# Interleaved hi and lo blocks, backward weight columns and a 64-byte shift in a PE-filled four-layer trunk

## The chip, the cores and the metric

The kernel runs on one core of a Trainium2 chip. The metric is the device time of one launch, in microseconds; less is better. Two timed runs of the kernel before took 2014.99 and 2016.04 us, a median of 2015.51 us.

## The reference

The input is one sequence of 256 frames with 2048 features. Two layers follow each other: a token mixer and an MLP in each, every one of the four behind an RMSNorm and with a residual add.

```python
for i in range(DEPTH):                         # DEPTH = 2
    h = rms_norm(x, norm_mix[i])
    x = x + (stick_breaking_mixer if i == 0 else dsa_mixer)(h, ...)   # 16 heads of 128
    h = rms_norm(x, norm_mlp[i])
    x = x + jnp.square(jax.nn.relu(h @ w_up[i])) @ w_down[i]          # 2048 -> 8192 -> 2048
```

The first mixer projects to q, k, v (2048 to 6144), weighs keys by stick breaking and projects back (2048 to 2048). The second projects to 16 query heads, 4 key and 4 value heads and an indexer (16 heads of 64), keeps the 64 best keys of each query, and projects back. Nearly all the arithmetic lies in the products of 256 frames with weight matrices; the inputs and the result are float32.

## The kernel before, in words

**Products.** Every float32 operand is split in two float32r parts, hi and lo, and a product is the sum of three: hi with hi, lo with hi, hi with lo. The frames are the stationary operand of TensorE (128 features by 128 frames, loaded by a LDWEIGHTS ahead of each MATMUL), the weight matrix is the moving one (128 features by 512 columns). One *item* is a block of 256 rows (KB = 2 k tiles of 128) by 512 columns of a weight matrix, 512 KB. An item in the plain form has 12 matmuls: 2 halves of the frames, 2 k tiles, 3 part products. A list of 882 items is worked off in order; each is loaded by SyncE into `wraw` (five buffers), split by ScalarE into `wh` (line 1327) and by VectorE into `wl` (line 1328), two items ahead of its matmuls.

**Where products stand.** `tokens_out` (matmuls in line 342, and in line 333 for the first two items) makes a group of 512 output columns from eight items, q = 0 to 7, of which q reads k tiles 2q and 2q + 1. There are 16 such groups over the normed features `xT` (four in the first mixer, two in each MLP, eight in the second mixer) and 8 in the two output projections, over `oT`. `seven_products` makes two columns of items at once: for some q a scheme of seven products in place of eight is used (line 465), and the others are plain products (line 446). With one set of the scheme these are q = 1, 3, 4, 5, 6, 7, with two sets q = 4 to 7; the k tiles from 8 on are never in the scheme, and `sums` adds up k tiles 0 to 7 alone. `xT` is the left operand of 18 such calls, four in the first mixer and seven in each MLP; 8 of them use one set and 10 two. The second product of an MLP reads the squared features from `half` (three buffers of 8 k tiles) and the sums of these from `S` and `S2`.

**Features.** `xT` has 16 k tiles; in each lie 256 hi values and then 256 lo values, so that a stationary block is 128 consecutive float32 values (512 bytes in a partition). They are written by ScalarE (hi) and VectorE (lo) with 256 values an instruction: `prep_first` (lines 188 and 189) for the first layer, `turn_steps` (lines 255 and 260) for the three later ones, at the seams between the four sections. The indexer's key product (`ki_part`, lines 1047 and 1048) is the one place where `xT` is the moving operand, with 80 weight columns as the stationary one.

**Addresses.** Some tiles named `pad` fill up space. With them the build puts `xT`, `wh`, `wl`, `wraw`, `half`, `S`, `S2`, `X`, `Y` and `Z` at multiples of 512 bytes in a partition. In the second mixer, `vh` and `vl` lie 128 bytes past such a multiple, and `ph` and `pl` 224 bytes past; `o_step` (lines 1244 to 1246) multiplies these.

Of the kernel before, what the change touches and what calls it, by code (L numbers as in the profile page):

```python
# [9 lines left out]
F32 = mybir.dt.float32  # L10
F32R = mybir.dt.float32r
BF16 = mybir.dt.bfloat16
AF = mybir.ActivationFunctionType
OP = mybir.AluOpType
# [3 lines left out]
P = 128  # L18
D = 2048
S = 256  # L20
KT = D // P
# [18 lines left out]
KB = WT // 512  # L40
# [15 lines left out]
BIAS = 60  # L56
ROLES = {
    "mixer": ("G0 H0 s1 G1 s3 H1 G2 s6 H2 s5 G3 s7 H3 s2 G4 H4 s4 G5 H5", dict(
        T1a=1, T2a=3, T3a=5, T4a=11, P1=5, P6=7, P5=10, P7=11)),
# [38 lines left out]
class Item:  # L98
# [3 lines left out]
    def __init__(self, src, a, b, mm):  # L102
        self.src, self.a, self.b, self.mm, self.post = src, a, b, mm, []
        self.form, self.early, self.alone, self.raw = None, [], False, None


@with_exitstack
def trunk(ctx, tc, x, x_t, gains_t, w_in_a, w_out_a, w_in_b, w_out_b, rel_bias, w_up, w_down, out):
# [6 lines left out]
    consts = ctx.enter_context(tc.tile_pool(name="consts", bufs=1))  # L115
# [6 lines left out]
    act, dve, pool, pe = nc.scalar, nc.vector, nc.gpsimd, nc.tensor  # L122
# [5 lines left out]
    def pin(ins):  # L128
        if pinned[0]:
            keep(ins)  # L130

    def copy(o, i, scale=1.0):
        pin(act.activation(o, i, AF.Copy, scale=scale))
# [22 lines left out]
    room = tmp.tile([P, 2 * P], F32, name="junk", bufs=1)  # L156
# [14 lines left out]


    xs = consts.tile([P, 2, D], F32, name="xs")
    xT = consts.tile([P, KT, 2, S], F32R, name="xT")
    ss = consts.tile([P, 2, 4], F32, name="ss")
    rs = consts.tile([P, 2], F32, name="rs")
    consts.tile([P, 106], F32, name="pad2")
# [4 lines left out]
    def prep_first(n, after=None):  # L182

        r = staged[n // 2][:, 2 * (n % 2):2 * (n % 2) + 2]
        for j in range(2):
            kt = 2 * n + j
            g = gains[:, kt:kt + 1]
            copy(xT[:, kt, 0, :], r[:, j, :], scale=g)
            pin(dve.scalar_tensor_tensor(xT[:, kt, 1, :], r[:, j, :], g,
                                         xT[:, kt, 0, :].bitcast(F32), op0=OP.mult,  # L190
                                         op1=OP.subtract))
            if after is not None:
                after(j)
# [51 lines left out]
    def turn_steps(c, col):  # L245

        def views():
            for j in range(4):
                kt = 4 * c + j
                h, l = (xT[:, kt, i, :].rearrange("p (t q) -> p t q", t=2) for i in range(2))  # L250
                yield j, gains[:, col + kt:col + kt + 1], h, l

        def high(z):
            for j, g, h, l in views():
                keep(act.activation(h, z.rearrange("p (t k) q -> p t k q", t=2)[:, :, j, :],
                                    AF.Copy, scale=g))

        def low(z):
            for j, g, h, l in views():
                keep(dve.scalar_tensor_tensor(  # L260
                    l, z.rearrange("p (t k) q -> p t k q", t=2)[:, :, j, :], g, h.bitcast(F32),
                    op0=OP.mult, op1=OP.subtract))

        return [xs[:, t, c * 512:(c + 1) * 512] for t in range(2)], high, low
# [44 lines left out]
    def rows(w, r0, nr, c0, ncol):  # L309
        return w[r0:r0 + nr, c0:c0 + ncol].rearrange("(a p) c -> p a c", p=P)  # L310

    def high_first(wh, wl, tokens=2):


        for parts in (((0, wh), (1, wh)), ((0, wl),)):
            for t in range(tokens):
                for j in range(KB):
                    for part, wx in parts:
                        yield (t, j, part, wx, wx is wh and (j, part) == (0, 0),
                               wx is wl and j == KB - 1)  # L320

    def tokens_out(items, key, w, r0, c0, lhs, q, done, alone=False):


        def first(wh, wl):

            acc = accp.tile([P, 2, 512], F32, name="acc")
            accs[key] = [acc[:, t, :] for t in range(2)]
            L = lhs()
            for j in range(KB):  # L330
                for n, (part, wx) in enumerate(((0, wh), (1, wh), (0, wl))):
                    for t in range(2):
                        pin(pe.matmul(accs[key][t], L[:, j, part, t * P:(t + 1) * P], wx[:, j, :],  # L333
                                      start=(j == 0 and n == 0), stop=False))

        def mm(wh, wl):
            if q == 0:
                acc = accp.tile([P, 2, 512], F32, name="acc")
                accs[key] = [acc[:, t, :] for t in range(2)]
            acc, L = accs[key], lhs()  # L340
            for t, j, part, wx, a, z in high_first(wh, wl):
                (keep if alone else pin)(pe.matmul(  # L342
                    acc[t], L[:, KB * q + j, part, t * P:(t + 1) * P], wx[:, j, :],
                    start=a and q == 0, stop=z and q == QB - 1))
        it = Item(rows(w, r0 + KB * P * q, KB * P, c0, 512), KB, 512,
                  mm if len(items) >= LEAD else first)
        it.alone = alone
        if q == QB - 1 and done is not None:
            it.post.append(lambda: done(accs.pop(key)))
        items.append(it)  # L350
# [65 lines left out]
    def seven_products(items, at, sec, w, r0, cols, left, role, S, last=False):  # L416

        base = len(items)
        keys = [("pair", base + i) for i in range(2)]
        order, place = ROLES[role]  # L420
        order = [name if name[0] != "s" else (name + "a")[:3] for name in order.split()]
# [129 lines left out]
    def mlp(l, next_col):  # L551
# [4 lines left out]
        def begin(pl):  # L556
            sec["pool"] = pl
            sec["E"] = pl.tile([P, 4, 512], F32, name="E", bufs=1)
            sec["Sx"] = pl.tile([P, 2, 2, 4 * KB, P], F32R, name="half", bufs=3)
            sec["Sh", 0] = pl.tile([P, 2, 4 * KB, P], F32R, name="S", bufs=1)  # L560
            for n in "ab":
                for name in "XYZ":
                    sec[n][name] = pl.tile([P, KB, 512], F32, name=name + n, bufs=1)
                sec[n]["new X"] = lambda X=sec[n]["X"]: X
# [107 lines left out]
        def up(role, f, n, taken=None, summed=None):  # L672
            keys, gather, base, ends = seven_products(
                items, at, sec, w_up[l], 0, [2048 * f + 1024 * n + 512 * c for c in range(2)],
                lambda: xT, role, lambda k: sec["Sx"][:, "ab".index(k)])
            place = ROLES[role][1]
            late = len(items)
# [24 lines left out]
        def down(role, f, n, taken=None, summed=None):  # L702
# [4 lines left out]
                lambda k: sec["Sh", "ab".index(k)], last)  # L707
            place = ROLES[role][1]

# [44 lines left out]
        if next_col is not None:  # L754
            at(BIAS, lambda: bias_rows(sec["pool"].tile([P, 512 + REL], F32, name="S2", bufs=1)))
            for n in range(HEADS):
                at(BIAS + 14 + 2 * n, bias_spread, n)
        for i in sorted(hooks):
# [9 lines left out]
    def mixer_a():  # L768
# [195 lines left out]
        for n in range(1, 8):  # L964
            at(FRONT * n - 3, prep_first, n)
# [24 lines left out]
    def bias_rows(room):  # L990

        rb, bv = room[:, :32], room[:, 512:512 + REL]
        keep(nc.scalar.dma_start(
            rb, rel_bias.unsqueeze(1).to_broadcast([HEADS, P // HEADS, 32])))
        for k, (lo, hi) in enumerate(zip(BUCKET_FROM, BUCKET_FROM[1:] + [256])):
            pool.tensor_copy(bv[:, 256 - hi:256 - lo], rb[:, k:k + 1].to_broadcast([P, hi - lo]))
            lo, hi = max(lo, 1), min(hi, 128)
            if lo < hi:  # L1000
                pool.tensor_copy(bv[:, 255 + lo:255 + hi],
                                 rb[:, 16 + k:17 + k].to_broadcast([P, hi - lo]))
        bias["rows"] = bv
# [5 lines left out]
    def mixer_b():  # L1009
# [27 lines left out]
        def qi_done(s, acc):  # L1037
            to_features(acc, lambda: st["qiT"][:, s], None)

        def ki_part(q):  # L1040
            def mm(wh, wl):
                if q == 0:
                    accs["ki"] = accp.tile([P, 2, 512], F32, name="acc")
                acc = accs["ki"]
                for j in range(8):
                    k = 8 * q + j
                    pe.matmul(acc[:80, 0, :], wh[:, j, :], xT[:, k, :, :], start=(k == 0), stop=False)  # L1047
                    pe.matmul(acc[:80, 0, 0:S], wl[:, j, :], xT[:, k, 0, :], start=False,
                              stop=(k == KT - 1))
            return Item(rows(w_in_b, 8 * P * q, 8 * P, 4096, 80), 8, 80, mm)  # L1050

# [199 lines left out]
        for s, q in side_by_side(2, QB):  # L1251
            tokens_out(items, ("qi", s), w_in_b, 0, 3072 + 512 * s, lambda: xT, q,
                       lambda acc, s=s: qi_done(s, acc))
# [44 lines left out]
    parts = {}  # L1298
# [35 lines left out]
    for i in range(1, RAW):  # L1334
        load(i)
    warm(WARM)
    prep_first(0, lambda j: split(0, slice(j, j + 1)))
    for i in range(LEAD):
        for a in parts_of(i)[:2 * i]:
# [51 lines left out]
```

## Time and profile before

| | |
|---|---|
| median of two timed runs | 2015.51 us |
| span of the profiled execution | 2013.3 us |
| PE, weight loads, DVE, ACT busy | 100%, 82%, 88%, 60% |
| matmuls, and weight loads | 8960 each |
| granted TensorE clock | 1.000 |
| DMA | 464.87 MB, 231 GB/s |

The profile gives the profiled execution's span from its first to its last instruction, 2013.3 us, and no other time of that execution; the median of the timed runs is 2.2 us longer, for what lies around it. [...]

### The profile page before, as it was taken

The numbers are of one execution on the slowest core, as the hardware profiler recorded it, in microseconds if no ns is written. First come the engines' busy times: TensorE is split into PE (matmuls) and PEld (weight loads), VectorE is DVE, ScalarE is ACT, GpSimd is POOL, SyncE is SP. The second block draws the span as 40 slices with busy tenths as digits, with TensorE's granted clock in tenths as the row PEclk, the third lists the DMA queues.
The fourth block names the chain that finished last, engine by engine and source line by source line (L and its number), as shares of the span: only waits on it lengthen the run. The fifth ranks groups of instructions, "written<-read, shape, count | busy, mean of one in ns | idle before, by whom it ended". The sixth has DMA issues, their size and how long they took to land.

```text
span 2013.3 us, 25248 instructions
## 1 busy us (share of the span) xinstructions
PE 2007.0 (100%) x8960; PEld 1658.8 (82%) x8960; DVE 1781.5 (88%) x1906; ACT 1209.5 (60%) x1437; POOL 37.8 (2%) x71
## 2 busy tenths in 40 slices
PE   9999999999999999999999999999999999999999
PEld 7888888888888888888888788888888888888887
DVE  6879866699889999999995898678999999999997
ACT  6567664566456656666564556555655665665753
POOL 0001110000200000000000000000000000000000
PEclk9999999999999999999999999999999999999999
DMA  9776756988888767886688698488876786698764
GB/s 317 229 239 173 218 205 175 288 232 255 231 267 242 225 219 220 255 249 227 191 247 260 197 261 262 153 241 265 254 230 214 217 248 217 218 264 216 262 196 160
DMA packets 477663, 464.87 MB, mean 231 GB/s; under 512 B 269856, under 2 KB 280160, under 8 KB 477536
## 3 DMA queue, kind: packets, MB, share of 16 engines
q1 hardware_dynamic: 469488, 455.81, 75.1%
q10 hardware_dynamic: 8048, 7.45, 1.1%
q8 instruction: 70, 1.15, 0.2%
q14 instruction: 57, 0.47, 0.1%
HBM read 425.90 MB, written 37.22 MB: 230 GB/s over the span
## 4 chain that ended last, share of the span: by engine, by line
PE 99%; DMA 1%; SPq 0%; DVE 0%; issue 0%; ACT 0%; DVEq 0%
PE acc L446 46%; PE acc L342 25%; PE aux L465 13%; PE acc L465 10%; PE acc L333 1%; PE aux L1194 1%; DMA qk<-td 0%; PE acc L868 0%; PE aux L928 0%; PE acc L1082 0%; DMA wraw<-in_w_in_a_dram 0%; SPq L220 0%; PE acc L1047 0%; PE aux L930 0%; PE acc L870 0%; DMA td<-jx 0%
## 5 line engine op out<-in xcount | busy, mean ns | idle before, releaser
L1327 ACT ACTIVATE wh<-wraw 128x1024 fp32r<-128x1024 f32 (+1 forms) x691 | 726.1, 1055 | 534.6 <-PE acc L446 274.5
L1328 DVE TENSOR_TENSOR wl<-wraw,wh 128x1024 fp32r<-128x1024 f32 (+1 forms) x691 | 832.0, 1215 | 161.2 <-ACT wh L1327 151.2
L446 PE MATMUL acc<-wh,xT 128*128 128x512 f32 x1408 | 348.4, 389 | 0.0
L446 PE MATMUL acc<-wh,half 128*128 128x512 f32 x1368 | 337.8, 389 | 0.0
L446 PEld LDWEIGHTS acc<-wh,xT 128*128 128x128 f32 x1408 | 263.7, 188 | 54.5
L446 PEld LDWEIGHTS acc<-wh,half 128*128 128x128 f32 x1368 | 256.8, 188 | 53.3
L342 PE MATMUL acc<-wh,xT 128*128 128x512 f32 x960 | 240.0, 391 | 0.0
L342 PEld LDWEIGHTS acc<-wh,xT 128*128 128x128 f32 x960 | 179.6, 188 | 38.9 <-issue 1.7
L446 PE MATMUL acc<-wl,xT 128*128 128x512 f32 x704 | 188.2, 389 | 0.0
L446 PE MATMUL acc<-wl,half 128*128 128x512 f32 x684 | 182.8, 389 | 0.0
L446 PEld LDWEIGHTS acc<-wl,xT 128*128 128x128 f32 x704 | 132.1, 188 | 27.5
L446 PEld LDWEIGHTS acc<-wl,half 128*128 128x128 f32 x684 | 128.4, 188 | 26.7
L342 PE MATMUL acc<-wl,xT 128*128 128x512 f32 x480 | 129.6, 391 | 0.0
L342 PEld LDWEIGHTS acc<-wl,xT 128*128 128x128 f32 x480 | 90.0, 188 | 19.3 <-DVE wl L1328 0.3
L1327 ACT ACTIVATE wh<-Za 128x1024 fp32r<-128x1024 f32 x60 | 63.6, 1060 | 51.7 <-DVE Za L522 16.8
L465 PE MATMUL aux<-wh,half 128*128 128x512 f32 x348 | 93.0, 389 | 0.0
L465 PE MATMUL aux<-wh,S 128*128 128x512 f32 x300 | 80.2, 389 | 0.0
L465 PEld LDWEIGHTS aux<-wh,half 128*128 128x128 f32 x348 | 65.3, 188 | 13.6
L1328 DVE TENSOR_TENSOR wl<-Za,wh 128x1024 fp32r<-128x1024 f32 x60 | 73.2, 1220 | 1.7 <-ACT wh L1327 0.6
L465 PE MATMUL acc<-wh,half 128*128 128x512 f32 x256 | 68.4, 389 | 0.0
L465 PEld LDWEIGHTS aux<-wh,S 128*128 128x128 f32 x300 | 56.3, 188 | 11.7
L342 PE MATMUL acc<-wh,oT 128*128 128x512 f32 x256 | 65.3, 392 | 0.0
(278 smaller groups left out, 2581.0 us busy)
## 6 DMA issues: line engine op xcount, KB each, us to landing
wraw<-in_w_down_dram SPq DMA_DIRECT2D x235, 512.0 KB, 4.7
wraw<-in_w_up_dram SPq DMA_DIRECT2D x234, 512.0 KB, 4.6
wraw<-in_w_in_a_dram SPq DMA_DIRECT2D x88, 512.0 KB, 4.9
wraw<-in_w_in_b_dram SPq DMA_DIRECT2D x64, 512.0 KB, 4.7
td<-jx SPq DMA_DIRECT2D x240, 128.0 KB, 4.4
jx<-td SPq DMA_DIRECT2D x45, 512.0 KB, 5.9
wraw<-in_w_out_a_dram SPq DMA_DIRECT2D x32, 512.0 KB, 4.2
wraw<-in_w_out_b_dram SPq DMA_DIRECT2D x32, 512.0 KB, 4.5
```

What stands on the lines that cost most here:

```text
L333: pin(pe.matmul(accs[key][t], L[:, j, part, t * P:(t + 1) * P], wx[:, j, :], start=(j == 0 and n == 0), stop=False))
L342: (keep if alone else pin)(pe.matmul(acc[t], L[:, KB * q + j, part, t * P:(t + 1) * P], wx[:, j, :], start=a and q == 0, stop=z and q == Q ...
L446: keep(pe.matmul(acc[:, t, :], L[:, KB * qs[i] + j, part, t * P:(t + 1) * P], wx[:, j, :], start=a and i == 0, stop=z and i == end - (last ...
L465: keep(pe.matmul(p, lhs(part, j), wx[:, j, :], start=to is None and a and n == sets[0], stop=to is None and z and n == sets[-1]))
L1194: pe.matmul(ps[:, h - lo, :], qT[:, GRP * t + h, :], kT[:, n, 0:w], start=True, stop=True)
L1327: order(act.activation(wh[:, a], raw[:, a], AF.Copy))
L1328: order(dve.tensor_sub(wl[:, a], raw[:, a], wh[:, a].bitcast(F32)))
```

## The change

1. `xT` is now read through a class `Blocks`. The k tiles 0 to 9 keep their layout. In k tiles 10 to 13 ("pairs") the hi and the lo value of a frame lie side by side; in k tiles 14 and 15 ("fours") four values lie together, hi and lo of frame q and of frame 128 + q. A stationary block there is 128 values 8 bytes or 16 bytes apart. In fours, the writers' instructions are 2 x 128 in form. For the last six k tiles the moving operand of `ki_part` is strided too.
2. In `tokens_out`, the items q = 4, 6 and 7 read the 512 weight columns from the last to the first, and write the sums in PSUM from the last to the first as well.
3. In the second MLP, 64 bytes lie ahead of `half` and 448 more behind `S`: `half` and `S` lie 64 bytes past a multiple of 512, and `X`, `Y`, `Z` and `S2` lie on multiples as before.

```diff
+FORMS = {4: "parts", 5: "pairs", 6: "pairs", 7: "fours"}
+BACK = (4, 6, 7)
+class Blocks:
+    def __init__(self, room):
+        self.room = room
+    def block(self, kt):
+        form = FORMS.get(kt // KB, "parts")
+        b = self.room[:, kt, :]
+        if form == "parts":
+            v = b.rearrange("p (i t q) -> p i t q", i=2, t=2)
+        elif form == "pairs":
+            v = b.rearrange("p (t q i) -> p i t q", i=2, t=2)
+        else:
+            v = b.rearrange("p (q t i) -> p i t q", i=2, t=2)
+        return v
+    def __getitem__(self, key):
+        p, k, part, ts = key
+        if isinstance(k, slice):
+            return self.room.rearrange("p k (i s) -> p k i s", i=2)[key]
+        return self.block(k)[:, part, ts.start // P, :]
...
-    xT = consts.tile([P, KT, 2, S], F32R, name="xT")
+    xT = Blocks(consts.tile([P, KT, 2 * S], F32R, name="xT"))
...
+            way = slice(None, None, -1 if q in BACK else 1)
             for t, j, part, wx, a, z in high_first(wh, wl):
                 (keep if alone else pin)(pe.matmul(
-                    acc[t], L[:, KB * q + j, part, t * P:(t + 1) * P], wx[:, j, :],
+                    acc[t][:, way], L[:, KB * q + j, part, t * P:(t + 1) * P], wx[:, j, way],
...
             sec["E"] = pl.tile([P, 4, 512], F32, name="E", bufs=1)
+            if next_col is None:
+                pl.tile([P, 16], F32, name="gap", bufs=1)
             sec["Sx"] = pl.tile([P, 2, 2, 4 * KB, P], F32R, name="half", bufs=3)
             sec["Sh", 0] = pl.tile([P, 2, 4 * KB, P], F32R, name="S", bufs=1)
+            if next_col is None:
+                pl.tile([P, 112], F32, name="gap2", bufs=1)
```

The instructions of all engines stand in the same order as before; their counts are the same, and only addresses, steps and two shapes differ. On ScalarE, at the seam ahead of the first MLP, the four writes of hi values of k tiles 12 to 15 stood so before, between splits of weights:

```order
L1327 ACTIVATE wh<-wraw 128x1024 x6
L255 ACTIVATE xT<-jx,gains 128x256 x4
L1327 ACTIVATE wh<-wraw 128x1024 x5
L408 ACTIVATE half<-Zb 128x1024
L1327 ACTIVATE wh<-wraw 128x1024
```

and stand so now, with every line number moved by the added code:

```order
L1358 ACTIVATE wh<-wraw 128x1024 x6
L280 ACTIVATE xT<-jx,gains 128x256 x2
L280 ACTIVATE xT<-jx,gains 128x2x128 x2
L1358 ACTIVATE wh<-wraw 128x1024 x5
L434 ACTIVATE half<-Zb 128x1024
```

Nothing moved there; the two writes of fours have another form.

More of the change, by code (lines that the diff above doesn't have):

```diff
@@ L187, in prep_first @@
             g = gains[:, kt:kt + 1]
-            copy(xT[:, kt, 0, :], r[:, j, :], scale=g)
-            pin(dve.scalar_tensor_tensor(xT[:, kt, 1, :], r[:, j, :], g,
-                                         xT[:, kt, 0, :].bitcast(F32), op0=OP.mult,
+            b, rj = xT.block(kt), r[:, j, :].rearrange("p (t q) -> p t q", t=2)
+            copy(b[:, 0], rj, scale=g)
+            pin(dve.scalar_tensor_tensor(b[:, 1], rj, g, b[:, 0].bitcast(F32), op0=OP.mult,
                                          op1=OP.subtract))
@@ L249, in views @@
                 kt = 4 * c + j
-                h, l = (xT[:, kt, i, :].rearrange("p (t q) -> p t q", t=2) for i in range(2))
+                h, l = (xT.block(kt)[:, i] for i in range(2))
                 yield j, gains[:, col + kt:col + kt + 1], h, l
@@ L1046, in mm @@
                     k = 8 * q + j
-                    pe.matmul(acc[:80, 0, :], wh[:, j, :], xT[:, k, :, :], start=(k == 0), stop=False)
-                    pe.matmul(acc[:80, 0, 0:S], wl[:, j, :], xT[:, k, 0, :], start=False,
+                    b = xT.block(k)
+                    pe.matmul(acc[:80, 0, :], wh[:, j, :], b, start=(k == 0), stop=False)
+                    pe.matmul(acc[:80, 0, 0:S], wl[:, j, :], b[:, 0], start=False,
                               stop=(k == KT - 1))
```

## The prediction

> **What bounds the kernel now.** I read the busy times and the clock first, then the chain of work that ended last, then TensorE's waits.
>
> ```profile
> PE 2007.0 (100%) x8960; PEld 1658.8 (82%) x8960; DVE 1781.5 (88%) x1906; ACT 1209.5 (60%) x1437; POOL 37.8 (2%) x71
> PEclk9999999999999999999999999999999999999999
> PE 99%; DMA 1%; SPq 0%; DVE 0%; issue 0%; ACT 0%; DVEq 0%
> PE acc L169 <- DVE ones L141: 1.1, 1, 1.1
> PE acc L333 <- ACT wh L1327: 0.7, 1, 0.7
> PE acc L868 <- DMA qk<-td: 0.4, 1, 0.4
> ```
>
> TensorE has something to do all the time, at the full clock, it makes 99% of the chain, and all its waits together are 2.2 us. What counts is therefore only how fast matmuls follow each other. In a view of the chain, long runs of equal matmuls are single rows:
>
> ```profile
> 701.10 16.32 PE acc L446 x72
> 1348.17 38.08 PE acc L342 x168
> 2007.91 0.28 PE L432 MATMUL acc<-wl,half 128*128 128x256 f32 x1
> 2009.11 0.28 PE L432 MATMUL acc<-wh,half 128*128 128x256 f32 x1
> ```
>
> 16.32 us over 72, and 38.08 us over 168, are both **226.7 ns from one start to the next**, with `half` and with `xT` as left operand. The last two rows, of the timeline at the program's end, are the first and the last of 11 successive starts with 256 columns: 1.20 us over 10 steps, 120 ns. 256 columns more cost 106.7 ns, so 512 columns cost 213.3 ns, and 13.3 ns are paid per matmul whatever its length. Nothing in this change can save more than these 13.3 ns of a matmul; what it can add is open. So the question is what a touched matmul's 226.7 ns becomes.
>
> **How many are touched.** The rows are of the view by stretches (whole program, then the second MLP), for one line or tile:
>
> ```profile
> 0.00:2014.00 2014.00, 512.57 (x2208) 412.54 (x2208) 1.00 0.76 231
> 0.00:2014.00 2014.00, 23.16 (x96) 17.87 (x96) 1.00 0.76 231
> 1384.00:2014.00 630.00, 344.64 (x1476) 276.27 (x1476) 30.31 (x25) 16.82 (x16) 1.00 0.74 225
> 1384.00:2014.00 630.00, 65.03 (x264) 49.55 (x264) 8.51 (x7) 7.35 (x7) 0.00 (x0) 1.00 0.74 225
> ```
>
> The first two are lines 342 and 333: 2304 matmuls of `tokens_out`, which is 24 groups of 8 items of 12. Three q of eight go backward: 24 x 3 x 12 = 864.
> Strided loads: the 16 groups on `xT` have 16 x 2 x 12 = 384 in pairs (q = 5, 6) and 16 x 12 = 192 in fours (q = 7); the 18 calls of `seven_products` on `xT` have two columns each, 18 x 2 x 2 x 12 = 864 in pairs and 432 in fours. Together **1248 in pairs, 624 in fours**. Of the 864 backward ones 192 + 192 are among these, and **480** are backward only.
> Shifted loads: the last two rows are the matmuls on `half` (1476) and on the sums (264) of the second MLP. 72 of the latter read `S2` (three calls with two sets, 4 x 6 each), which stays on a multiple of 512 bytes: 1476 + 192 = **1668**.
>
> **Does a load's own length matter?** The groups of weight loads by shape, and four fp32 matmuls of the timeline:
>
> ```profile
> L446 PEld LDWEIGHTS acc<-wh,xT 128*128 128x128 f32 x1408 | 263.7, 188 | 54.5
> L1047 PEld LDWEIGHTS acc<-xT,wh 128*80 128x80 f32 x16 | 2.4, 148 | 1.3
> 113.77 0.38 PE L870 MATMUL acc<-qk 128*128 128x128 f32 x2
> 113.98 0.60 PE L868 MATMUL acc<-qk 128*128 128x256 f32 x2
> ```
>
> 48 columns more make a load 40 ns longer, 0.83 ns each: 128 columns stream in 107 ns, and the other 81 ns are latency. The two matmuls of line 870, with a load each, take 0.21 us from 113.77 to 113.98, so a load and a matmul fit in some 107 ns. At a pitch of 226.7 ns a load may therefore stream at half speed (213 ns) and stay hidden; at a quarter of it (427 ns) it would set the pitch. By length alone, strides cost nothing up to a factor of two.
>
> **Does a load disturb the running matmul?** Every operand of the 226.7 ns runs lies on a multiple of 512 bytes. Line 1244 to 1246 do not, and they come here behind a settled stream, with no gap:
>
> ```profile
> 1238.19 1.98 PE L342 MATMUL acc<-wh,xT 128*128 128x512 f32 x8
> 1240.91 0.40 PE L342 MATMUL acc<-wh,oT 128*128 128x512 f32 x1
> 1241.14 0.40 PE L1244 MATMUL aux<-ph,vh 128*128 128x512 f32 x1
> ...
> 1242.31 0.40 PE L1246 MATMUL aux<-ph,vl 128*128 128x512 f32 x1
> 1242.55 1.30 PE L342 MATMUL acc<-wh,oT 128*128 128x512 f32 x5
> ```
>
> From 1238.19 to 1240.91 there are 12 steps of 226.7 ns. From 1241.14 to 1242.55 there are 6 of **235 ns**. Same shapes, same clock; other addresses (load 128, moving operand 224 bytes past a multiple). So the 13.3 ns are not fixed: they were 21.7 there. The indexer's matmuls, whose loads have 80 columns and lie 320 bytes apart, say what they grow with:
>
> ```profile
> 1087.42 0.40 PE L1047 MATMUL acc<-xT,wh 128*80 128x512 f32 x1
> 1092.31 0.39 PE L1047 MATMUL acc<-xT,wh 128*80 128x512 f32 x1
> ```
>
> There are 14 pairs of 512 and 256 columns in 4.89 us, 349.3 ns each: 29.3 over the 320 of the columns, 14.6 per matmul. Against 21.7 that is 0.68; 80 against 128 columns is 0.63. The surplus seems to go with what a load reads while a matmul streams.
>
> [...]
>
> **The sum.** Bounds and values for each kind, in ns per matmul:
>
> - *Shifted loads, 1668.* Between -13.3 (the surplus vanishes) and +8.3 (the row of line 1244). One operand is off here, and by 64 bytes, where two were off in that row: I take half, +4.1. 1668 x 4.1 = 6.8 us.
> - *Strided loads, 1872.* They start on or near a multiple and then walk through 1 or 2 KB in place of 512 bytes, so that they keep no fixed place beside the moving operand. Between -13.3 and, if the surplus went with the stretch of memory that a load walks, +13.3 for pairs and +40 for fours (1024 and 2048 bytes against 512: twice and four times 13.3). I take the one measured value for loads out of step, +8.3: 15.5 us.
> - *Backward only, 480.* The same 2 KB is read from the other end; one operand starts elsewhere: +4.1, 2.0 us. Bounds -13.3, and +213.3 if reading or writing backward halved the rate; line 868's fp32 matmuls show what half the rate is (256 columns at 0.22 us, in the row 113.98 with 0.44 to the next line at 114.42).
> - *The indexer.* 12 matmuls have a strided moving operand: 0 to 1.9 us (all columns at half speed); at +8.3, 0.1 us.
>
> The row that ends that step:
>
> ```profile
> 114.42 0.38 PE L870 MATMUL acc<-qk 128*128 128x128 f32 x2
> ```
>
> Writing `xT` with strides: ScalarE and VectorE have 24 strided writes each (16 pairs, 8 fours).
>
> ```profile
> L255 ACT ACTIVATE xT<-jx,gains 128x256 fp32r<-128x256 f32 x48 | 20.4, 496 | 0.7 <-DMA jx<-td 0.7
> L260 DVE SCALAR_TENSOR_TENSOR xT<-jx,gains,xT 128x256 fp32r<-128x256 f32 x48 | 20.0, 478 | 0.0
> 200.00:400.00 200.00, 199.64 (x911) 166.19 (x910) 136.88 (x146) 115.25 (x148) 13.34 (x20) 1.00 0.72 220
> 1000.00:1200.00 200.00, 200.00 (x925) 162.26 (x924) 160.71 (x265) 113.34 (x204) 0.00 (x0) 1.00 0.82 236
> ```
>
> If each took twice as long, that is 24 x 0.5 = 12 us on either engine, 3 us at each of four seams. Around the seams VectorE is busy 137 and 161 us of 200 (the third busy time of a row), ScalarE less; no wait of TensorE names `xT`. Taken as 0. Were that cover gone, the split of the next weights (line 1328) would be late by up to 3 us a seam, 12 us in all. DMA issues, SyncE and GpSimd are untouched.
>
> Together 6.8 + 15.5 + 2.0 + 0.1 = 24.4 us on the span of 2013.3: 2037.7, and with the 2.2 us between that span and the median, **2040 us**, 1.2% slower. With half of the sum this case gives 2028, and with line 1244's 8.3 ns for all 4020 touched matmuls (33.4 us) 2049.
>
> **Rivals.**
>
> - *Nothing changes (2012 to 2022).* A stream of equal steps may settle at 226.7 ns at any phase, as it does for `half` and `xT` alike; line 1244's six matmuls have no two neighbours with the same addresses, and so may never have settled. For it: the two long runs are equal to 0.1 ns. Against it: the surplus was another at once when the addresses were. [...]
> - *The surplus goes with the stretch that a load walks (2064 and more).* Pairs walk twice 512 bytes, fours four times: 1248 x 13.3 + 624 x 40 = 41.6 us, with the shift 48.4: 2064. If it starts from 21.7 ns out of step, 1248 x 30 + 624 x 73 = 83 us, with the shift at 13.8, 2112. For it: 0.68 against 0.63 above. Against it: contiguous loads cannot tell bytes walked from columns read.
> - *Backward reading or writing runs at half rate.* 864 x 213.3 = 184 us: 2200. Nothing in the trace goes backward; all sums are written upward. It decides from any loss over 47 ns a matmul (2%).
> - *Fours load at a quarter rate.* 427 ns of streaming, and a step as long: 624 x 200 = 125 us, 2140. For and against it there is no row; it decides from a load over twice as slow.
> - *Faster: the load falls out of the matmul's way.* The streams read 9.6 bytes a ns (moving) and 4.8 (a contiguous load). Pairs make the load's walk as fast as the moving one's; if they start apart they stay apart, and 13.3 ns go. With the shift and the backward reads doing the same, 4020 x 13.3 = 53 us: 1962; pairs alone 17 us, 1999. It decides when the mean of the touched steps falls under 226.7. Against it: the only other addresses in the trace were slower.
>
> [...]
>
> That the change does not do what it says can be left aside: the program's order is the same and the steps of the operands are in it.
>
> **How the numbers follow.** Chances: forecast 0.34; nothing 0.24; walked stretch 0.22; faster 0.08; backward at half rate 0.08; fours at a quarter rate 0.04; together 1. About 2% (40 us) is what a measurement of this kernel can tell from no change. Faster by more needs nearly all 53 us: 0.02. Slower by more, over 2056, are the walked stretch and both rate cases: 0.34. The rest, 0.64, is within 2%. The range leaves out both rate cases (0.12), the upper part of the walked stretch (0.05) and the better half of faster (0.03): 2004 to 2090. Cases of both signs hold the chance, but the likeliest one's own range is 2028 to 2049.
>
> **What would show it.** Runs of line 368 and 472 in the new trace (342 and 446 before) have a step for each kind: q = 4 backward only, q = 5 pairs, q = 6 both, q = 7 fours and backward; and `half` in the first MLP stands against `half` in the second. 235 ns in pairs and fours, 231 in the second MLP's `half`, 226.7 in the first's, would bear the sum out. I am wrong if k tiles 10 to 15 step at 226.7, if fours differ from pairs, or if q = 4 is far from 227. Waits of TensorE for `wl` or `xT` at the seams would show that the cover of the writes was too thin.

## The result, and the profile after

The changed kernel took **2045.92 us** (median of two runs, 2045.53 to 2046.32) against 2015.51: ratio 1.0149, 95% interval 1.012 to 1.0179. Slower by 30 us, at the same granted clock of 1.000. The span of its profiled execution is 2043.8 us, 30.5 more than the 2013.3 of before. All times here and below are of executions at that clock; one of the four of `e1_shift`, at 0.556 and 3400.13 us, is left out.

The page's busy times, its row of granted clock and its shares of the chain, and then the two largest rows of TensorE's waits, are the first thing to set beside those of before:

```profile
PE 2037.8 (100%) x8960; PEld 1698.0 (83%) x8960; DVE 1787.4 (87%) x1906; ACT 1211.7 (59%) x1437; POOL 38.5 (2%) x71
PEclk9999999999999999999999999999999999999999
PE 99%; DMA 0%; SPq 0%; ACT 0%; DVE 0%; DVEq 0%; issue 0%
PE acc L194 <- DVE ones L166: 1.1, 1, 1.1
PE acc L358 <- ACT wh L1358: 0.9, 2, 0.5
```

TensorE's busy time rose by 30.8 us (2007.0 to 2037.8), which is all of the difference. It still makes 99% of the chain, and no new wait has come up: none names `xT`, and the split of the weights (line 1358) holds it for 0.9 us in all. So the time lies in the steps from one matmul to the next, and there I looked for it. A row of the timeline lasts longer than a step: in the trace of before the mean row of line 446 on `xT` lasts 389 ns while the matmuls start 226.7 ns apart. So steps are read from starts. In the timeline of TensorE in one group of `tokens_out` (line 368; columns: start, us, the instruction, how many in a row) each item begins with eight matmuls on `wh`, and the distance between two such rows is one item of 12:

```profile
1153.71 2.03 PE L368 MATMUL acc<-wh,xT 128*128 128x512 f32 x8
1156.52 1.98 PE L368 MATMUL acc<-wh,xT 128*128 128x512 f32 x8
1159.24 1.98 PE L368 MATMUL acc<-wh,xT 128*128 128x512 f32 x8
...
1164.68 1.98 PE L368 MATMUL acc<-wh,xT 128*128 128x512 f32 x8
1167.40 2.03 PE L368 MATMUL acc<-wh,xT 128*128 128x512 f32 x8
1170.20 2.03 PE L368 MATMUL acc<-wh,xT 128*128 128x512 f32 x8
1173.00 2.03 PE L368 MATMUL acc<-wh,xT 128*128 128x512 f32 x8
```

q = 0 (from 1156.52) and q = 3 (from 1164.68) take 2.72 us, 226.7 ns a step as before. q = 4, backward only (from 1167.40), and q = 5, pairs (from 1170.20), take 2.80 us: 233.3 ns. q = 7 of the group before, fours and backward (from 1153.71), takes 2.81 us: 234. Two rows of the chain stand for the third edit, 72 steps on `half` in the first MLP and in the second:

```profile
707.63 16.32 PE acc L472 x72
1687.85 16.80 PE acc L472 x72
```

16.32 us are 226.7 ns a step, 16.80 us are 233.3. And two starts in a row of items with fours in `seven_products`, in the timeline:

```profile
1861.92 2.04 PE L472 MATMUL acc<-wh,xT 128*128 128x512 f32 x8
...
1864.74 1.57 PE L472 MATMUL acc<-wh,xT 128*128 128x512 f32 x6
```

2.82 us for 12, 235.0 ns. **Three different edits give nearly the same step**, 6.6 to 8 ns over the old one. Set matmul by matmul against the trace of before, where they start in the same order, the start times say what each kind added: the 1668 with shifted loads 10.9 us, the 1872 with strided ones 13.4, the 480 backward only 2.9, the indexer 2.0, and the untouched matmuls 1.3, nearly all of it in the first ten steps behind a touched one. That is the 30.5 us of the span.

The indexer's last matmuls in the timeline, with strided moving operand, the first two rows on a k tile in pairs and the others on fours:

```profile
1101.74 0.64 PE L1078 MATMUL acc<-xT,wh 128*80 128x512 f32 x1
1102.20 0.41 PE L1079 MATMUL acc<-xT,wl 128*80 128x256 f32 x1
1102.43 0.65 PE L1078 MATMUL acc<-xT,wh 128*80 128x512 f32 x1
1102.88 0.42 PE L1079 MATMUL acc<-xT,wl 128*80 128x256 f32 x1
1103.12 0.65 PE L1078 MATMUL acc<-xT,wh 128*80 128x512 f32 x1
```

From start to start 512 columns take 0.46 us in pairs and 0.45 in fours, and 256 take 0.23 and 0.24: half the rate, some 0.69 us for the two matmuls of a k tile where they took 0.349 before. Six k tiles are 6 x 0.34 = 2.0 us.

The other engines. The group of loads in line 472 by shape (count, busy us, mean ns, idle), the writers of `xT` as a tile's rows (min/median/max ns), and the busy times in the stretch from 200 to 400 us (TensorE, loads, VectorE, ScalarE, GpSimd):

```profile
L472 PEld LDWEIGHTS acc<-wh,xT 128*128 128x128 f32 x1408 | 283.8, 215 | 44.1
L280 ACT ACTIVATE xT<-jx,gains x48: 491/495/764, 359.7 to 1379.6; 128x256 fp32r<-128x256 f32 x48
L285 DVE SCALAR_TENSOR_TENSOR xT<-jx,gains,xT x48: 476/480/710, 363.5 to 1383.8; 128x256 fp32r<-128x256 f32 x48
200.00:400.00 200.00, 200.00 (x905) 168.04 (x904) 137.49 (x147) 113.27 (x144) 13.37 (x20) 1.00 0.73 219
```

The mean load of this group rose from 188 to 215 ns: the trace has the contiguous ones at 188, pairs at 193 and 608 of all 624 fours at 308 to 313. The medians of the writes, 495 and 480 ns, lie within 2 ns of those of before (495 and 478); pairs take 501 to 528 ns on ScalarE and 476 to 484 on VectorE in the trace, and only fours are much dearer, 724 to 783 and 681 to 729, and VectorE's 137 us in that stretch, around a seam, are those of before.

### The profile page after: what moved, and what is told of

It is laid out like the page before. It is cut to its first block, busy times and chain, and to the rows that moved or that the text cites. A ratio compares the mean times of both kernels' runs of the same rounds, so it can differ in the third digit from the quotient of the medians.

```text
span 2043.8 us, 25250 instructions
## 1 busy us (share of the span) xinstructions
PE 2037.8 (100%) x8960; PEld 1698.0 (83%) x8960; DVE 1787.4 (87%) x1906; ACT 1211.7 (59%) x1437; POOL 38.5 (2%) x71
## 4 chain that ended last, share of the span: by engine, by line
PE 99%; DMA 0%; SPq 0%; ACT 0%; DVE 0%; DVEq 0%; issue 0%
PE acc L472 47%; PE acc L368 25%; PE aux L491 13%; PE acc L491 10%; PE acc L358 1%; PE aux L1225 1%; PE acc L898 0%; PE aux L958 0%; PE acc L1113 0%; PE acc L1078 0%; DMA wraw<-in_w_in_a_dram 0%; PE aux L960 0%; PE acc L900 0%; PE aux L1275 0%; PE acc L458 0%; PE aux L1262 0%
## 5 line engine op out<-in xcount | busy, mean ns | idle before, releaser
L472 PE MATMUL acc<-wh,xT 128*128 128x512 f32 x1408 | 355.2, 394 | 0.0
L472 PE MATMUL acc<-wh,half 128*128 128x512 f32 x1368 | 342.3, 392 | 0.0
L472 PEld LDWEIGHTS acc<-wh,xT 128*128 128x128 f32 x1408 | 283.8, 215 | 44.1
L368 PE MATMUL acc<-wh,xT 128*128 128x512 f32 x960 | 243.5, 395 | 0.0
L368 PEld LDWEIGHTS acc<-wh,xT 128*128 128x128 f32 x960 | 188.7, 206 | 34.8 <-issue 2.0
L472 PE MATMUL acc<-wl,xT 128*128 128x512 f32 x704 | 191.3, 393 | 0.0
L472 PEld LDWEIGHTS acc<-wl,xT 128*128 128x128 f32 x704 | 143.4, 215 | 22.2
L368 PE MATMUL acc<-wl,xT 128*128 128x512 f32 x480 | 131.3, 395 | 0.0
L368 PEld LDWEIGHTS acc<-wl,xT 128*128 128x128 f32 x480 | 95.1, 206 | 17.0 <-DVE wl L1359 0.3
L491 PEld LDWEIGHTS aux<-wh,half 128*128 128x128 f32 x348 | 65.3, 188 | 14.6
L491 PE MATMUL acc<-wh,half 128*128 128x512 f32 x256 | 69.3, 392 | 0.0
```

What stands on the lines that cost most here:

```text
L368: (keep if alone else pin)(pe.matmul(acc[t][:, way], L[:, KB * q + j, part, t * P:(t + 1) * P], wx[:, j, way], start=a and q == 0, stop=z ...
L472: keep(pe.matmul(acc[:, t, :], L[:, KB * qs[i] + j, part, t * P:(t + 1) * P], wx[:, j, :], start=a and i == 0, stop=z and i == end - (last ...
L491: keep(pe.matmul(p, lhs(part, j), wx[:, j, :], start=to is None and a and n == sets[0], stop=to is None and z and n == sets[-1]))
```

## The experiments

My theory after the result: the step is 226.7 ns only where a load and the running matmul read memory in one fixed relation, and anything that breaks it costs 6 to 8 ns. The rivals: each edit has a cost of its own (a strided load, a backward read or write, an address that is not a multiple of 512 bytes), or an address counts by itself. Each single run stands against a run of the kernel before on the same chip (2014.91 to 2015.37 us). Steps are item or run lengths over their counts, or, where said, means over all such matmuls in the trace.

### Each edit alone

The kernel of `e1_shift` is the changed one with

```diff
-FORMS = {4: "parts", 5: "pairs", 6: "pairs", 7: "fours"}
-BACK = (4, 6, 7)
+FORMS = {}
+BACK = ()
```

> The kernel before with the third edit alone: half and S of the second MLP 64 bytes past a multiple of 512. Theory 'settled stream' (a stream keeps the 226.7 ns step only when the load and the moving operand are both contiguous, forward and congruent; any other stream steps at about 233.3 ns): 1668 touched matmuls at 233.3 ns, all others at 226.7; 1668 x 6.6 = 11.0 us, so 2026.5 us. Rival 'the edits need each other' (the shift alone costs nothing because only the mixture of different streams next to each other unsettles them): half of the second MLP at 226.7 ns, 2015.5 us.

It took 2026.74 to 2027.19 us against 2015.37 (nine runs), ratio 1.0057 [1.0037, 1.0077]. Its chain, `half` in the first and in the second MLP:

```profile
701.10 16.32 PE acc L472 x72
1671.25 16.80 PE acc L472 x72
```

226.7 and 233.3 ns: a shift of the loads by 64 bytes, with nothing strided or backward in the program, costs 6.6 ns.

`e2_forms` keeps `FORMS`, has `BACK = ()` and no gaps.

> The kernel before with the first edit alone: k tiles 10 to 13 in pairs, 14 and 15 in fours. Theory 'settled stream': pairs and fours step alike, near 233.5 to 234, 1872 x 7 = 13 us, 2028.5 us. Rival 'the surplus goes with the stretch that a load walks': pairs at 240 ns, fours at 267 ns, 1248 x 13.3 + 624 x 40 = 41.6 us, 2057 us.

2030.87 us, ratio 1.0077 [1.0062, 1.0092]. Timeline of one group, from q = 4 (contiguous) over q = 5 and 6 (pairs) to q = 7 (fours):

```profile
1166.25 1.98 PE L368 MATMUL acc<-wh,xT 128*128 128x512 f32 x8
1168.97 2.03 PE L368 MATMUL acc<-wh,xT 128*128 128x512 f32 x8
1171.77 2.03 PE L368 MATMUL acc<-wh,xT 128*128 128x512 f32 x8
1174.58 2.28 PE L368 MATMUL acc<-wh,xT 128*128 128x512 f32 x9
```

226.7, then 2.80 and 2.81 us: 233.3 and 234 ns. Over the whole trace pairs step at 233.2 ns in the mean and fours at 234.9. Fours walk twice as far as pairs and their load takes 310 ns in place of 193; the step shows under 2 ns of that. In pairs the lo values begin 4 bytes past the hi values, and so off the multiple, which costs something by itself (232.4 ns at 4 bytes in the map of distances below). But the last four matmuls of an item, on `wl`, load hi values alone, which begin on a multiple, and they step at 233.2 to 233.4 too: the stride has a cost of its own. Matmul by matmul the strided ones added 13.0 us to the trace of before, the indexer 2.0 and the others 0.7, together the 15.6 us by which the span grew (15.5 between the medians).

`e3_back` has `FORMS = {}`, keeps `BACK`, and has no gaps.

> The kernel before with the second edit alone: the items q = 4, 6 and 7 of tokens_out read their weight columns and write their sums backward, 864 matmuls. Theory 'settled stream': 233.3 ns each, 864 x 6.6 = 5.7 us, 2021.2 us. Rival 'backward is free, what the whole change shows for q = 4 comes from its neighbours': 226.7 ns once four or five matmuls of an item are through, under 2 us, 2016 to 2017.5 us.

2020.98 us, ratio 1.003 [1.0018, 1.0042]. Timeline, q = 4 (backward), q = 5 (forward), q = 6 (backward):

```profile
1161.12 2.03 PE L368 MATMUL acc<-wh,xT 128*128 128x512 f32 x8
1163.92 1.99 PE L368 MATMUL acc<-wh,xT 128*128 128x512 f32 x8
1166.66 2.03 PE L368 MATMUL acc<-wh,xT 128*128 128x512 f32 x8
```

2.80, then 2.74 us: 233.3 backward, and 228 in the forward item that follows, whose first steps still carry some of it (its first eight take 1.83 us, 228.8 ns each). The three parts cost 11.6 (by the middle run, 2026.96), 15.5 and 5.6 us, 32.7 together, against 30.4 for the whole change. 384 matmuls are strided and backward at once, and in the trace of the whole change these step at 233.8 ns, no slower than those that are only strided (233.7 in pairs, 235.0 in fours). The second disturbance of a matmul is free, so 384 x 6.6 ns = 2.5 us are counted twice, and 30.2 remain.

### Which address counts

`e6_moving` is `e1_shift` with the moving operands 64 bytes off as well:

```diff
-    tmp.tile([P, 96], F32, name="pad", bufs=1)
+    tmp.tile([P, 80], F32, name="pad", bufs=1)
...
+    wpool.tile([P, 16], F32, name="gapw", bufs=1)
```

> As with the third edit alone, and wh and wl (the moving operand) 64 bytes past a multiple of 512 as well. Theory 'only the distance between load and moving operand counts': the products on half and S of the second MLP, where both are 64 bytes past, go back to 226.7 ns, and all others, with the load on a multiple and the moving operand 64 past, step at 233.3: some 6900 x 6.6 = 45 us, 2061 us. Rival 'the load alone must lie on a multiple of 512': half and S of the second MLP at 233.3 and all others at 226.7, 2026.5 us. Second rival 'both must lie on a multiple': all at 233.3, 8600 x 6.6 = 57 us, 2072 us.

2031.06 us, not the 2061 of the first theory. In the second MLP `half` and `wh` are now both 64 bytes past a multiple of 512; in the first only `wh` is. The chain, first MLP and second:

```profile
706.91 16.48 PE acc L472 x72
1681.55 16.32 PE acc L472 x72
```

The second MLP's `half` is back at 226.7 ns, and the first's, on a multiple as ever, went to 228.9. So no address counts by itself: the **distance from the moving operand to the load** does. It has a sign, since +64 costs 6.6 ns and -64 costs 2.2 here and 2.6 in the mean over the trace; at that price the other matmuls add some 16 us and not 45.

`e4_off_a`, `e5_off_b`, `e8_off_c` and `e9_off_d` map the distance. `xT` lies as before, contiguous and read forward, but the k tiles of q = 4 to 7 lie some bytes later:

```diff
+OFFS = {4: 4, 5: 8, 6: 32, 7: 64}        # float32 values; e4_off_a
...
+        at = 2 * S * kt + OFFS.get(kt // KB, 0)
+        return self.room[:, at:at + 2 * S].rearrange("p (i t q) -> p i t q", i=2, t=2)
```

with `{4: 1, 5: 2, 6: 48, 7: 96}` in `e5_off_b`, `{4: 12, 5: 24, 6: 40, 7: 60}` in `e8_off_c` and `{4: 3, 5: 52, 6: 56, 7: 62}` in `e9_off_d`.

> The kernel before with the layout of xT as it was, but the k tiles read by q = 4, 5, 6 and 7 lying 16, 32, 128 and 256 bytes past a multiple of 512 (all tiles behind xT move by 512 bytes). The moving operand stays on a multiple, so these are the distances from moving operand to load. Theory 'the cost grows with the distance': 16 and 32 bytes step between 226.7 and 230 ns, 128 and 256 at 233 or more. Rival 'anything but a multiple of 512 unsettles alike': all four at 229 to 234 ns, 1344 plain loads (192 and 432 with q = 4 to 7 in each) x 2 to 7 ns, 2020 to 2030 us in all. Third 'there are distances better than none': one of the four under 226 ns.

> As the run with 16, 32, 128 and 256 bytes, with 4, 8, 192 and 384 bytes. Theory 'the cost grows with the distance': 4 and 8 bytes at 226.7 ns (they start within the same 64 bytes as the moving operand), 192 at 233, and 384, which is 128 short of the next multiple, near the 229 ns that 64 short has shown. Rival 'anything but a multiple unsettles alike': all four at 229 to 234 ns. Third 'there are distances better than none': one of the four under 226 ns.

> The runs so far gave, for the distance from moving operand to load: 0, 16 and 256 bytes 226.7 to 227 ns, 4 bytes 232, 8 bytes 231, 32 and 64 bytes 233, 128 and 384 bytes 232, 192 and 448 bytes 229. Here q = 4, 5, 6, 7 have 48, 96, 160 and 240 bytes. Theory 'the distance counts modulo 256 bytes': 240 stands for 16 short of a multiple and, if the good place is a point, steps at 229 or more; 48, 96 and 160 lie between 229 and 234. Rival 'the good place is a span of some 32 bytes around zero': 240 at 226.7. Third 'there are distances better than none': one of the four under 226 ns.

> As the run with 48, 96, 160 and 240 bytes, with 12, 208, 224 and 248 bytes. Theory 'only places 16 bytes apart can settle': 12 and 248 at 229 or more, as 4 and 8 were, 208 and 224 at 227 to 229. Rival 'the nearer to zero, the better': 12 and 248 at 227, 208 and 224 at 229. Third 'there are distances better than none': one of the four under 226 ns.

They took 2023.35, 2027.40, 2028.34 and 2027.35 us. Timeline of `e4_off_a` (q = 4, 5, 6 and 7 at 16, 32, 128 and 256 bytes), and, from an earlier group of the same trace, q = 7 and the q = 0 that follows it:

```profile
1147.21 1.98 PE L361 MATMUL acc<-wh,xT 128*128 128x512 f32 x8
1149.93 1.98 PE L361 MATMUL acc<-wh,xT 128*128 128x512 f32 x8
...
1160.82 1.98 PE L361 MATMUL acc<-wh,xT 128*128 128x512 f32 x8
1163.54 2.02 PE L361 MATMUL acc<-wh,xT 128*128 128x512 f32 x8
1166.34 2.02 PE L361 MATMUL acc<-wh,xT 128*128 128x512 f32 x8
1169.13 2.25 PE L361 MATMUL acc<-wh,xT 128*128 128x512 f32 x9
```

16 bytes: 2.72 us, nothing lost. 32 bytes: 2.80. 128 bytes: 2.79. 256 bytes: 2.72 (from 1147.21). In `e8_off_c`, q = 7 (240 bytes) with the q = 0 after it, and q = 4, 5 and 6 (48, 96, 160):

```profile
1150.17 1.98 PE L361 MATMUL acc<-wh,xT 128*128 128x512 f32 x8
1152.90 1.98 PE L361 MATMUL acc<-wh,xT 128*128 128x512 f32 x8
...
1163.78 2.03 PE L361 MATMUL acc<-wh,xT 128*128 128x512 f32 x8
1166.58 2.03 PE L361 MATMUL acc<-wh,xT 128*128 128x512 f32 x8
1169.39 2.02 PE L361 MATMUL acc<-wh,xT 128*128 128x512 f32 x8
```

240 bytes takes 2.73 us, within 0.01 of 0 and 256; 48 and 96 bytes take 2.80 and 2.81. Mean steps by distance over all these matmuls of the four traces, with 64 from `e1_shift` and 448 (-64) from `e6_moving`:

| bytes | ns | bytes | ns | bytes | ns |
|---|---|---|---|---|---|
| 0 | 226.7 | 48 | 233.4 | 224 | 233.2 |
| 4 | 232.4 | 64 | 233.3 | 240 | 227.0 |
| 8 | 230.7 | 96 | 234.7 | 248 | 233.4 |
| 12 | 227.9 | 128 | 232.3 | 256 | 227.0 |
| 16 | 227.0 | 160 | 233.3 | 384 | 232.5 |
| 32 | 233.4 | 192 | 228.9 | 448 | 229.0 to 229.3 |
| | | 208 | 231.9 | | |

As far as these distances tell, they count modulo 256 bytes: 128 and 384 agree (232.3 and 232.5 ns), 192 and 448 (228.9, and 229.0 to 229.3), 0 and 256 (226.7 and 227.0). The fast step stands at 0 and at 16 bytes to either side (227.0 at 16 and at 240, which is -16); 12 nearly has it (227.9). The cost does not grow with the distance: 4 bytes cost more than 16 (232.4 ns against 227.0), and the places between cost 1 to 8 ns and not always the 6 to 8 of the theory. Of 19 distances none is under 226.7. The order between the others (192 at 229, 248 at 233) no theory of mine gives.

`e11_near` uses the map to forecast: in the first MLP `half` and `S` lie 32 bytes later, in the second 256.

```diff
+            gap = 8 if next_col is not None else 64
+            pl.tile([P, gap], F32, name="gap", bufs=1)
...
+            pl.tile([P, 128 - gap], F32, name="gap2", bufs=1)
```

> The kernel before with half and S 32 bytes past a multiple of 512 in the first MLP and 256 past in the second (S2, X, Y, Z on multiples). Theory 'the distance counts modulo 256 bytes, and 0 and 16 to either side settle': half and S of the second MLP at 226.7 ns, those of the first at 233.4; some 1690 x 6.7 = 11.3 us, 2026.7 us. Rival 'what counts is a multiple of 512, and the 256 bytes of xT were luck': both at 231 to 233.4, 2035 us or more.

2026.72 us against 2014.91 on that chip. Its chain, first MLP and second:

```profile
705.61 16.80 PE acc L472 x72
1678.23 16.32 PE acc L472 x72
```

The places have changed: 233.3 ns in the first MLP with 32 bytes, 226.7 in the second with 256. A shift four times as long as that of the change costs nothing, one of half its length costs the same as it.

### Reading backward or writing backward

`e7_apart` (from `e3_back`) splits the direction in two:

```diff
+READ = (6, 7)
+WRITE = (4, 7)
...
-                    acc[t][:, way], L[:, KB * q + j, part, t * P:(t + 1) * P], wx[:, j, way],
+                    acc[t][:, out_way], L[:, KB * q + j, part, t * P:(t + 1) * P], wx[:, j, way],
```

> The second edit taken apart, with the rest as in the kernel before: in tokens_out the items q = 4 write their sums backward but read forward, q = 6 read backward but write forward, q = 7 do both (the columns of a group are then summed up in mixed order, so the output is another). Theory 'load and moving operand must walk together': q = 4 at 226.7 ns, q = 6 and 7 at 233.3; 2 x 288 x 6.6 = 3.8 us, 2019.2 us. Rival 'the write into PSUM is what costs': q = 4 and 7 at 233.3, q = 6 at 226.7, 2019.2 us too, told apart by the steps.

2018.71 us. Timeline from q = 4 (writes backward) over q = 5 (neither) and q = 6 (reads backward) to q = 7 (both):

```profile
1157.89 1.98 PE L369 MATMUL acc<-wh,xT 128*128 128x512 f32 x8
1160.62 1.98 PE L369 MATMUL acc<-wh,xT 128*128 128x512 f32 x8
1163.34 2.03 PE L369 MATMUL acc<-wh,xT 128*128 128x512 f32 x8
1166.14 2.27 PE L369 MATMUL acc<-wh,xT 128*128 128x512 f32 x9
```

2.73, 2.72 and 2.80 us: writing the sums backward is free, reading the weights backward costs 6.6 ns. All of the second edit's cost comes with the reads: 233.3 ns a step at q = 6 and 227.5 at q = 4. Whether it is the direction is not told apart from the start: a backward read begins at the last column, 2044 bytes into its block, and by start addresses the load then lies 4 bytes past it modulo 256, a place that costs 5.7 ns in the map (232.4) with both operands rising.

### Does the surplus go with what a load reads?

`e10_cols` takes the kernel before and loads fewer frames in three of the eight items:

```diff
+FRAMES = {4: 96, 5: 64, 6: 32}
...
+            m = FRAMES.get(q, P)
-                    acc[t], L[:, KB * q + j, part, t * P:(t + 1) * P], wx[:, j, :],
+                    acc[t][:m], L[:, KB * q + j, part, t * P:t * P + m], wx[:, j, :],
```

> The kernel before, but in tokens_out the items q = 4, 5 and 6 load and multiply only the first 96, 64 and 32 frames of each half of 128 (so the other frames miss these parts of their sums); the moving operand keeps its 512 columns. Theory 'the surplus over 213.3 ns goes with what a load reads': 13.3 x 96/128 = 10.0, 6.7 and 3.3 ns, so steps of 223.3, 220.0 and 216.7 ns. Rival 'the surplus is a fixed price of a load': 226.7 ns in all three. With 288 matmuls each: 5.8 us less or nothing, 2009.7 or 2015.5 us.

2017.95 us, not faster. Timeline from q = 4 to q = 7, and the loads by shape:

```profile
1157.56 2.00 PE L344 MATMUL acc<-wh,xT 128*96 128x512 f32 x8
1160.32 2.00 PE L344 MATMUL acc<-wh,xT 128*64 128x512 f32 x8
1163.08 2.02 PE L344 MATMUL acc<-wh,xT 128*32 128x512 f32 x8
1165.86 2.22 PE L344 MATMUL acc<-wh,xT 128*128 128x512 f32 x9
L344 PEld LDWEIGHTS acc<-wh,xT 128*96 128x96 f32 x128 | 20.6, 161 | 8.3
L344 PEld LDWEIGHTS acc<-wh,xT 128*64 128x64 f32 x128 | 17.2, 134 | 12.0
L344 PEld LDWEIGHTS acc<-wh,xT 128*32 128x32 f32 x128 | 13.8, 108 | 15.4 <-issue 0.3
```

The loads got shorter as the prediction's 0.83 ns a column has it (161, 134, 108 ns), but the step got longer: 2.76, 2.76 and 2.78 us an item, 230, 230 and 231.7 ns. Neither theory forecast that. With a load of a quarter of the columns (108 ns), at the best distance, a matmul still steps at 231.7 ns; the size of what the load reads is not what the surplus goes with. These matmuls also write fewer partitions of PSUM, so whether the load or the write lengthens the step is open.

## Why the prediction was right, and where it was not

The time of 2045.92 us lies 6 us above the forecast of 2040 and inside the likeliest case's own range, near the end that priced every touched matmul as line 1244's (2049). Part of the nearness is luck: the strided term was 2.1 us too large, and it covered some of what the shift (4.1), the backward reads (0.9), the indexer (1.9) and the untouched matmuls (1.3, which had no term) lacked.

- **What bounds the kernel.** Right: the busy time of TensorE took all of the difference, and no new wait came of the writes or the splits.
- **The counts.** Borne out: 1668, 1872 and 480 matmuls make up 27.2 of the 30.5 us.
- **Shifted loads.** Right in kind, size off: +6.6 ns measured for +4.1, 10.9 us for 6.8. I had halved line 1244's surplus because one operand was off there where two had been. `e6_moving` shows that reasoning to be wrong: two operands off by the same 64 bytes cost nothing (226.7 ns), and what counts is their distance. Line 1244's was 128 - 224 = -96 bytes, 160 modulo 256, and 160 steps at 233.3 in `e8_off_c`; its row was the right price for this term too, near enough. The row itself was read a little high, from times rounded to 10 ns: all 34 unbroken steps of lines 1244 to 1246 in that trace have a mean of 233.9 ns, +7.2 and not +8.3.
- **Strided loads.** Right in kind and nearly in size: +7.2 ns for +8.3, 13.4 us for 15.5. Pairs and fours were to cost the same, and do but for 1 to 2 ns. The reason given, that such a load keeps no fixed place beside the moving operand, is not shown.
- **Backward only.** +6.6 ns once settled, 2.9 us for 2.0. Half the price was chosen for the same wrong reason as with the shift.
- **The indexer.** 2.0 us for 0.1. I took the step out of phase where the bound, all its columns at half speed, is what came: a moving operand 8 bytes apart is read at half the rate (0.45 against 0.23 us for 512 columns).
- **Writes of `xT`.** Right at 0: pairs cost the writers next to nothing (at most 528 ns on ScalarE and 484 on VectorE against medians of 495 and 478 before), fours some 0.25 us an instruction, and VectorE, busy 137 us of 200 around a seam, has room for them: no wait of TensorE names `xT`.
- **Length of a load.** Right, nearly: fours take 310 ns in place of 188. Less the prediction's 81 ns of latency that is an estimated 229 ns of streaming, far from the 427 that a quarter of the rate would take, and the step shows 1 to 2 ns of it. Pairs are as good as free for the load itself (193 ns against 188). For the indexer's moving operand they are not: there pairs are at half the rate already (0.46 us for 512 columns).
- **"The surplus seems to go with what a load reads."** Wrong, by `e10_cols`; no term of the sum rested on it, but the walked-stretch rival did. The indexer's loads, 320 bytes apart, lay at distances of 0, 64, 128 and 192 bytes modulo 256, so their 14.6 ns mixed the length of a load with its place.

The rivals. *Nothing changes* fell at once, though with a distance of 256 bytes (`e11_near`) it would have held for the shift. The step changes with the distance between the two operands' addresses (226.7 to 234.7 ns), so the load and the running matmul are not independent of each other. Where in the chip the two meet is not shown. *The walked stretch* fell with pairs and fours at one price; *half rate backward* and *a quarter rate for fours* with 233 ns and with loads of 310; *faster* with no kind, and none of 19 distances, under 226.7.

**What stays open.** Why the step is 226.7 ns at a few distances and 229 to 235 at the others is not shown. The equal steps seem to be a state that load and matmul fall into: in the traces the first ten or so steps after a break of the stream vary between 224 and 238 ns before they settle, in the trace of before again and again in the same order (235, 233, 236, 224, 231, 236, 228, 233, 230, then 227), and fewer columns, a stride, another direction or another distance all keep them from it. That is argued, not shown. A load that runs backward was not tried, which would tell whether two operands in the same direction settle again; nor was a backward read that starts at another distance, which would tell direction from start.

## What to carry to other kernels

Where TensorE never waits, and each matmul has a load of its own, look at the step from start to start in long runs of equal rows, not at busy shares: a surplus of 6.6 ns on 226.7 is 2.9% of the time, and no wait shows it. Lay the load and the moving operand out with one distance modulo 256 bytes (here 0, or 16 to either side, 226.7 to 227.0 ns), keep both contiguous and rising (8 bytes apart stepped at 233.2, weights read back at 233.3), and put a pad where a buffer breaks that. And price a disturbance at the one measured row, rather than at a share of it chosen by an argument: both halved terms were too small.

## What the runs showed of the hardware that I had not expected

- The step of a 512-column float32r matmul with its own 128-column load depends on the distance between the two operands in a partition, in these runs modulo 256 bytes and with a sign: 226.7 to 227.0 ns at 0, 16 and 240, 228.9 at 192, 230.7 at 8, 233.3 at 64, 234.7 at 96.
- Matmuls with a shorter load, and as many fewer partitions written, had a longer step: 230.0, 230.0 and 231.7 ns with 96, 64 and 32 columns against 226.7 with 128.
- Sums written to PSUM from the last column back cost nothing (2.73 us an item of 12 against 2.72); weights read back, from a start 4 bytes off the multiple of 256, cost 6.6 ns a matmul.
- A stationary operand with values 8 bytes apart loads in 193 ns (188 contiguous), with 16 bytes in 310; a moving one 8 bytes apart already halves the rate (0.46 us for 512 columns against 0.23).
